# The start of a decoder trunk reordered: x loaded first, products on ones ahead, v's products sorted by part

## The chip, the cores and the metric

The kernel runs on one core of one Trainium2 chip. The metric is the device time of one execution in microseconds (us). Before the change it is 1229.62 us, the median of three runs (1229.15 to 1229.67).

## What is computed

The reference is a trunk of two layers on 512 tokens of width 1024, all in float32. Layer 0 mixes tokens by an attention with forget gates, layer 1 by a gated short convolution; each mixer is followed by a squared-ReLU MLP and a gated per-layer input. Only the very beginning of layer 0 bears on the change:

```python
def rmsnorm(x, g):
    y = x * rsqrt(mean(x * x, axis=-1) + RMS_EPS)
    return y * g

hn = rmsnorm(x, g[0])                 # x: (512, 1024)
proj = hn @ w_attn_in                 # (512, 3*1024 + 16): q, k, v and 16 forget-gate logits
f_logit = proj[..., 3 * D:] + b_f     # 16 heads
```

The order in which q, k, v and the logits are computed is free. The kernel begins with a part of v and the logits.

## The kernel before

**Precision.** TensorE multiplies in a reduced float format (fp32r). To keep float32 accuracy the kernel splits each operand into a high part (rounded by a copy on ScalarE, `wh`, `hTh`) and a low part (what the rounding left, by a subtraction on VectorE or GpSimd, `wl`, `hTl`). `split` (L270) does both. A product is then three: high by high, low rows by high weights, high rows by low weights (`mm3`, L264 to L266).

**Blocks.** The 512 tokens are four blocks of 128 rows (t = 0 to 3), the width is eight blocks of 128 (k = 0 to 7). Each block of x comes as two halves of 128x512 (tiles `xa` for t = 0, `xc` for the others).

**The beginning, per token block.** `stats` squares both halves on ScalarE (L295, with a sum) and calls `rstd` on GpSimd (L287 adds, L290 raises to -1/2). `scaled` (L303) multiplies a half by that and by the gain `g0` on VectorE, giving `n_h`. `turned` (L312) transposes four 128x128 pieces of `n_h` on TensorE into the PSUM tile `n_p`. `keep` splits that into `hTh` (ScalarE) and `hTl` (VectorE), the turned rows. The gain `g0` is a row of 1024 numbers; two products with a one-row stationary of ones (L983) spread it over 128 partitions in PSUM.

**v.** The columns of v and of the logits are computed in three chunks (`V_CHUNKS`): first the last 256 columns of v with the 16 logit columns (272 wide), then 512, then 256. `values(c, t)` computes chunk c for token block t: eight k, three products each. Within it, after five k (`if k == 5 and between`), the next block's rows are turned. `keep_v` moves the result out of PSUM: the logits plus `b_f` on VectorE (L454), then the parts of v as high copies (ScalarE) and low parts (VectorE), one after the other.

**Loads.** `fetch` issues weight loads on SyncE's queue into a ring of 14 `raw` tiles; `prepare(n)` splits the weights up to number n (the first eight are those of the first chunk, 272 wide). `load_x` loads x. Loads complete on a ring of eight semaphores (DMAHW0 to DMAHW7), so the ninth load waits for the first to have landed, and so on.

**Order.** The program is ordered by a scheduler, except where a `manual_schedule` block fixes the order of the named engines as written: the loads (SyncE, ScalarE) and the first chunk of v (TensorE, VectorE, ScalarE). Each engine works through its own queue strictly in order.

## Time and profile before

| | |
|---|---|
| median of three runs | 1229.62 us |
| profiled execution | 1230.79 us |
| its span | 1229.1 us |
| granted clock, mean over the span | 0.997 |
| TensorE busy | 1210.3 us |
| VectorE, ScalarE, GpSimd busy | 912.2, 676.4, 657.1 us |
| instructions | 18662 |

The profile is of one execution. Its span runs from the first to the last instruction on the engines; the execution's own time is a little longer, and lies above the median of the runs beside it. In the rows, PE is TensorE, PEld its weight loads, DVE VectorE, ACT ScalarE, POOL GpSimd, SP SyncE; SPq and ACTq are the queues that issue loads. A row of the timeline gives start, length (us), engine, line, operation, what is written and read, and in brackets how long the engine was idle before and who released it. A group row gives busy time and the mean of one in ns. The lines are those of the kernel before.

### The profile page before, as it was taken

How to read it: one execution, taken by the hardware profiler on the slowest of the kernel's cores; microseconds unless marked ns; L12 is line 12 of the kernel's file. 1: busy time of each engine (PE TensorE's matmuls, PEld its weight loads, DVE VectorE, ACT ScalarE, POOL GpSimd, SP SyncE). 2: the span in 40 equal slices, each digit the busy share in tenths (PEclk: the TensorE clock that was granted, in tenths of full speed). 3: DMA queues.
4: the chain of work that ended last, by engine and by line, in shares of the span. 5: the costliest groups of instructions: out<-in, count | busy, mean ns of one | idle time of the engine just before them, and what ended most of it. 6: DMA issues, size and time to landing. Idle time of an engine off the chain costs nothing.

```text
span 1229.1 us, 18662 instructions
## 1 busy us (share of the span) xinstructions
PE 1210.3 (98%) x6188; PEld 1030.5 (84%) x6188; DVE 912.2 (74%) x1410; ACT 676.4 (55%) x1429; POOL 657.1 (53%) x619
## 2 busy tenths in 40 slices
PE   7999999999999999999999999999999999999997
PEld 6888888898888888888889999989888888888886
DVE  5648878676778767869877798867776787669873
ACT  5447777556744654455565544445756345645551
POOL 2016656244977787775213255316677878678210
PEclk9999999999999999999999999999999999999999
DMA  7456564542343324428133033552422443236401
GB/s 251 149 157 172 143 172 113 167 149 78 103 137 105 98 73 137 132 68 296 57 100 108 30 104 95 156 174 74 137 78 60 137 138 99 64 113 180 162 18 52
DMA packets 85793, 148.73 MB, mean 121 GB/s; under 512 B 10112, under 2 KB 17328, under 8 KB 85696
## 3 DMA queue, kind: packets, MB, share of 16 engines
q1 hardware_dynamic: 85488, 147.27, 39.2%
q8 instruction: 49, 0.80, 0.3%
q14 instruction: 48, 0.39, 0.1%
q10 hardware_dynamic: 144, 0.26, 0.1%
q0 software_dynamic: 64, 0.00, 0.0%
HBM read 136.93 MB, written 6.37 MB: 117 GB/s over the span
## 4 chain that ended last, share of the span: by engine, by line
PE 96%; ACT 1%; DVE 1%; DMA 1%; issue 1%; POOL 1%; SPq 0%; DVEq 0%; POOLq 0%; ACTq 0%
PE up L266 9%; PE up L265 9%; PE up L264 9%; PE dn L264 8%; PE dn L265 8%; PE dn L266 8%; PE qk L265 2%; PE qk L264 2%; PE qk L266 2%; PE pg L265 2%; PE pg L264 2%; PE pg L266 2%; PE n_p L312 1%; PE pT L539 1%; PE v L264 1%; PE v L265 1%
## 5 line engine op out<-in xcount | busy, mean ns | idle before, releaser
L273 DVE TENSOR_TENSOR wl<-raw,wh 128x512 fp32r<-128x512 f32 (+1 forms) x398 | 377.3, 991 | 22.3 <-ACT wh L272 21.3
L272 ACT CAST wh<-raw 128x512 fp32r<-128x512 f32 (+1 forms) x398 | 217.5, 620 | 4.6 <-DVE xd L348 4.4
L265 PE MATMUL up<-hTh,wl 128*128 128x512 f32 (+1 forms) x576 | 210.2, 365 | 0.0
L266 PE MATMUL up<-hTl,wh 128*128 128x512 f32 (+1 forms) x576 | 209.7, 366 | 0.0
L264 PE MATMUL up<-hTh,wh 128*128 128x512 f32 (+1 forms) x576 | 208.7, 366 | 0.0
L820 ACT ACTIVATE r<-up 128x512 f32<-128x512 f32 (+1 forms) x72 | 39.4, 547 | 203.2 <-PE up L266 201.0
L273 POOL TENSOR_TENSOR wl<-dn_T,wh 128x512 fp32r<-128x512 f32 x96 | 132.6, 1413 | 30.1 <-ACT wh L272 30.1
L167 POOL TENSOR_TENSOR dn_T<-raw,raw 128x512 f32<-128x512 f32 x56 | 86.9, 1563 | 68.8 <-DMA raw<-in_wdn 58.3
L265 PEld LDWEIGHTS up<-hTh,wl 128*128 128x128 f32 x576 | 108.6, 189 | 17.5
L264 PEld LDWEIGHTS up<-hTh,wh 128*128 128x128 f32 x576 | 108.6, 189 | 17.6
L266 PEld LDWEIGHTS up<-hTl,wh 128*128 128x128 f32 x576 | 108.3, 189 | 17.5
L866 DVE TENSOR_TENSOR acc<-dn,acc 128x512 f32<-128x512 f32 x168 | 107.3, 679 | 14.9 <-PE dn L266 14.8
L167 POOL TENSOR_TENSOR dn_T<-raw,dn_T 128x512 f32<-128x512 f32 x56 | 92.4, 1650 | 2.2
L272 ACT CAST wh<-dn_T 128x512 fp32r<-128x512 f32 x112 | 61.4, 616 | 11.1 <-POOL dn_T L167 11.1
L273 DVE TENSOR_TENSOR A12l<-q,A12h 128x512 fp32r<-128x512 f32 x28 | 22.4, 801 | 55.0 <-ACT A12h L272 54.9
L880 POOL TENSOR_TENSOR acc<-acc,acc 128x512 f32<-128x512 f32 x28 | 46.9, 1706 | 9.9 <-DVE acc L866 9.9
L265 PE MATMUL qk<-hTh,wl 128*128 128x512 f32 x128 | 51.0, 399 | 0.0
L266 PE MATMUL qk<-hTl,wh 128*128 128x512 f32 x128 | 51.0, 398 | 0.0
L264 PE MATMUL qk<-hTh,wh 128*128 128x512 f32 x128 | 50.9, 398 | 0.0
L265 PE MATMUL pg<-wh,hTl 128*128 128x512 f32 x128 | 50.5, 394 | 0.0
L264 PE MATMUL pg<-wh,hTh 128*128 128x512 f32 x128 | 50.4, 394 | 0.0
L273 DVE TENSOR_TENSOR A11l<-q,A11h 128x256 fp32r<-128x256 f32 x28 | 23.1, 825 | 36.5 <-ACT A11h L272 36.5
(371 smaller groups left out, 3244.4 us busy)
## 6 DMA issues: line engine op xcount, KB each, us to landing
raw<-in_wup SPq DMA_DIRECT2D x128, 256.0 KB, 2.9
raw<-in_wdn SPq DMA_DIRECT2D x128, 256.0 KB, 2.8
raw<-in_wcq SPq DMA_DIRECT2D x36, 256.0 KB, 2.8
raw<-in_wqk SPq DMA_DIRECT2D x32, 256.0 KB, 3.4
raw<-in_wpg SPq DMA_DIRECT2D x32, 256.0 KB, 4.3
g<-in_g SPq DMA_DIRECT2D x22, 256.0 KB, 5.3
prl<-neg_c SPq DMA_DIRECT2D x16, 256.0 KB, 6.7
raw<-in_wo SPq DMA_DIRECT2D x16, 256.0 KB, 5.9
```

Of the source, the lines that this page charges most:

```text
L167: ins = nc.gpsimd.tensor_tensor(out=B[name], in0=B[a], in1=B[b], op=op)
L264: nc.tensor.matmul(ps, a.hi, b.hi, start=start, stop=False)
L265: nc.tensor.matmul(ps, a.lo, b.hi, start=False, stop=False)
L266: nc.tensor.matmul(ps, a.hi, b.lo, start=False, stop=stop)
L272: nc.scalar.copy(hi, src)
L273: return eng.tensor_tensor(out=lo, in0=src, in1=hi.bitcast(F32), op=ALU.subtract)
L312: nc.tensor.transpose(ps[:, j * P : (j + 1) * P], h[:, j * P : (j + 1) * P], ident)
L539: nc.tensor.transpose(ps[:, b * P : (b + 1) * P], probs[h][b][:, j * P : (j + 1) * P], ident)
L820: nc.scalar.activation(r[:, :n], ps[:, :n], AF.Relu)
L866: ins = nc.vector.tensor_tensor(out=a, in0=banks[s], in1=a, op=ALU.add)
L880: nc.gpsimd.tensor_tensor(out=a, in0=a, in1=acc[i, s][:, :S], op=ALU.add)
```

## The change

Only the beginning is touched, to the end of the first chunk of v, and `keep_v`.

- The load of `b_f` moves from the head of SyncE's queue to behind all of x. The two rows of the gain go from GpSimd's queue to ScalarE's, behind x's half there.
- A tile `warm` is set to one on VectorE, and `work(n)` issues n products of it with itself into a PSUM bank that nobody reads: eleven ahead of the gain's products, two between the two turned halves of block 0.
- Of the two halves that a mean of squares needs, ScalarE squares the first and VectorE the second (`products`, a product with a sum that starts at EPS); VectorE adds the two and GpSimd raises to -1/2 (`mean_squares`, `inverse`).
- The low parts of weights 2 and 3, 4 to 6, and 8 to 13 are computed on GpSimd rather than VectorE (`prepare(..., nc.gpsimd)`).
- In the first chunk the products are sorted by part: for k = 0 to 3 high by high, high rows by low weights, low rows by high weights; for k = 4 to 7 high by high, low rows, then (after the next block's rows are turned) low weights.
- `keep_v` issues all high copies first and then all low parts; the evacuation of block t is placed behind the products of block t + 1, and behind the scaled rows of later blocks.

SyncE's queue at the program's start, with what a load waits for, before and now (`xa` is x's block 0, `xc` with the lower numbers is block 1, `raw` are weights of v):

```order
L604 DMA b_f<-in_bf 128x16
L357 DMA xa_0_93<-in_x 128x512
L157 DMA raw_97<-in_wv 128x272
L157 DMA raw_99<-in_wv 128x272
L157 DMA raw_101<-in_wv 128x272
L157 DMA raw_103<-in_wv 128x272
L357 DMA xc_0_105<-in_x 128x512
L357 DMA xc_1_106<-in_x 128x512 [waits DMAHW0_49]
L157 DMA raw_109<-in_wv 128x272 [waits DMAHW1_49]
```
```order
L365 DMA xa_0_93<-in_x 128x512
L157 DMA raw_99<-in_wv 128x272
L157 DMA raw_101<-in_wv 128x272
L157 DMA raw_103<-in_wv 128x272
L157 DMA raw_105<-in_wv 128x272
L365 DMA xc_0_107<-in_x 128x512 [waits DMAHW0_49]
L365 DMA xc_1_108<-in_x 128x512 [waits DMAHW1_49]
L157 DMA raw_111<-in_wv 128x272 [waits DMAHW2_49]
L157 DMA raw_113<-in_wv 128x272 [waits DMAHW3_49]
```

`b_f` is gone from the front, and the loads of x's block 1 now wait for semaphores that block 0's loads hold (ScalarE's three loads take semaphores of the same ring).

ScalarE's queue at the start, before and now (`junk,n_q` are the squares with their sum, `wh` casts of weights, `hTh` casts of turned rows of block 0):

```order
L357 DMA xa_1_94<-in_x 128x512
L295 ACT_TABLE_LOAD
L295 ACTIVATE junk,n_q_0_155<-xa_0_93 128x512
L295 ACTIVATE junk,n_q_0_157<-xa_1_94 128x512
L272 CAST wh_163<-raw_97 128x272
L272 CAST wh_167<-raw_99 128x272
L272 CAST wh_171<-raw_101 128x272
L272 CAST wh_179<-raw_103 128x272
L272 CAST hTh<-n_p_0_183 128x4x128
L272 CAST wh_190<-raw_109 128x272
```
```order
L365 DMA xa_1_94<-in_x 128x512
L1023 DMA row_89<-in_g 1x512
L1023 DMA row_90<-in_g 1x512
L295 ACT_TABLE_LOAD
L295 ACTIVATE junk,n_q_0_172<-xa_0_93 128x512
L272 CAST wh_181<-raw_99 128x272
L272 CAST wh_185<-raw_101 128x272
L272 CAST wh_189<-raw_103 128x272
L272 CAST wh_193<-raw_105 128x272
L295 ACTIVATE junk,n_q_1_201<-xc_0_107 128x512
L272 CAST hTh<-n_p_0_208 128x4x128
L272 CAST hTh<-n_p_1_217 128x4x128
```

One square of block 0 left; the square of block 1 (`n_q_1`) stands ahead of block 0's `hTh` casts, and no weight is cast between those two any more.

VectorE around the third and fourth token block, before and now (`n_h` scaled rows of block 3, `hTl` low turned rows, `logit` block 0's logits, `v_3` low parts of v):

```order
L303 SCALAR_TENSOR_TENSOR n_h_0_284<-xc_0_121,n_r_y,g_0_126 128x512
L303 SCALAR_TENSOR_TENSOR n_h_1_286<-xc_1_122,n_r_y,g_1_127 128x512
L273 TENSOR_TENSOR hTl<-n_p_0_304,hTh 128x4x128
L273 TENSOR_TENSOR hTl<-n_p_1_311,hTh 128x4x128
L273 TENSOR_TENSOR wl_328<-raw_329,wh_327 128x512
L273 TENSOR_TENSOR wl_334<-raw_335,wh_333 128x512
L273 TENSOR_TENSOR wl_340<-raw_341,wh_339 128x512
L454 TENSOR_TENSOR logit<-v_0_237,b_f 128x16
L273 TENSOR_TENSOR v_3_135<-v_0_237,v_3_135 128x2x64 x2
```
```order
L311 SCALAR_TENSOR_TENSOR n_h_0_358<-xc_0_123,n_r_305,g_0_130 128x512
L311 SCALAR_TENSOR_TENSOR n_h_1_360<-xc_1_124,n_r_305,g_1_131 128x512
L470 TENSOR_TENSOR logit<-v_0_255,b_f 128x16
L485 TENSOR_TENSOR v_3_153<-v_0_255,v_3_153 128x2x64 x2
L273 TENSOR_TENSOR hTl<-n_p_0_400,hTh 128x4x128
L273 TENSOR_TENSOR hTl<-n_p_1_407,hTh 128x4x128
L470 TENSOR_TENSOR logit<-v_1_319,b_f 128x16
```

The low splits of 512-wide weights are gone from here, and the logits of block 0 stand directly behind block 3's scaled rows; the high copies of v on ScalarE wait for them.

```diff
--- before.py
+++ after.py
@@ -171,7 +171,7 @@
                     mybir.DependencyInfo(mybir.DependencyClass.Sync, mybir.DependencyReason.DATA),
                 )
 
-    def prepare(upto):
+    def prepare(upto, lows=None):
         while begun[0] < min(upto, len(order)):
             n = begun[0]
             begun[0] += 1
@@ -185,7 +185,7 @@
                 eng = nc.gpsimd if (key[0] == "dn" and key[2] > 0) or key[-1] in ON_POOL else nc.vector
             else:
                 fetch(at + 1)
-                raw, eng, w = fetched[at], nc.vector, loads[at].shape[-1]
+                raw, eng, w = fetched[at], lows or nc.vector, loads[at].shape[-1]
                 fetched[at] = None
             split(hi[:, :w], lo[:, :w], raw[:, :w], eng)
             ready[key] = Pair(hi[:, :w], lo[:, :w])
@@ -295,6 +295,14 @@
         nc.scalar.activation(junk, src, AF.Square, scale=D**-0.5, accum_out=ss)
         return ss
 
+    def products(src, name):
+        ss = stat(name)
+        nc.vector.tensor_tensor_reduce(
+            out=page(f"{name}_sq")[:, :S], in0=src, in1=src, scale=1.0 / D, scalar=EPS,
+            op0=ALU.mult, op1=ALU.add, accum_out=ss,
+        )
+        return ss
+
     def stats(t, xs, name):
         return rstd([squares(xs[n][:, :S], f"{name}_q{n}_{t}") for n in range(2)], f"{name}_r{t}")
 
@@ -385,9 +393,7 @@
                          f"{kind}r")
                 then(t)
 
-    def attention(hT, first_x, g0, by_hand):
-        b_f = consts.tile([P, H], F32, tag="bf", name="b_f")
-
+    def attention(hT, first_x, g0, b_f, work, by_hand):
         vs = [[page(f"v{t}_{i}", F32R) for i in range(4)] for t in range(NB)]
         n_f = NB * H
         logit = stat("logit", n_f)
@@ -435,7 +441,7 @@
                 )
                 nc.sync.dma_start(neg_c[b, :, :n], t[:H, :n])
 
-        def values(c, t, soon=SOON, between=None):
+        def values(c, t, mid=None):
 
             c0, width = V_CHUNKS[c]
             n_v = min(width, D - c0)
@@ -444,10 +450,20 @@
                 if width == 256:
                     w = wide("v", c, k // 2).at(lambda u: u[:, k % 2 * 256 : k % 2 * 256 + 256])
                 else:
-                    w = wide("v", c, k, soon=soon)
-                if k == 5 and between:
-                    between()
-                mm3(ps[:, :width], tokens(hT, k, t), w, k == 0, k == KT - 1)
+                    w = wide("v", c, k, soon=0 if mid else SOON)
+                if not mid:
+                    mm3(ps[:, :width], tokens(hT, k, t), w, k == 0, k == KT - 1)
+            HH, LH, HL = ("hi", "hi"), ("lo", "hi"), ("hi", "lo")
+            for n in range(2 if mid else 0):
+                for part, of in (HH, HL, LH) if n == 0 else (HH, LH, HL):
+                    if n and of == "lo":
+                        mid()
+                    for k in range(4 * n, 4 * n + 4):
+                        nc.tensor.matmul(
+                            ps[:, :width], getattr(tokens(hT, k, t), part),
+                            getattr(ready["v", c, k], of),
+                            start=k == 0 and part == of, stop=k == KT - 1 and of == "lo",
+                        )
 
             def keep_v():
                 if n_v < width:
@@ -455,13 +471,20 @@
                         out=logit[:, t * H : (t + 1) * H], in0=ps[:, n_v:width], in1=b_f,
                         op=ALU.add,
                     )
+                splits = []
                 for c1 in range(0, n_v, 256):
                     src = ps[:, c1 : c1 + 256].rearrange("p (i e d) -> p i e d", e=2, d=HD)
                     block = vs[t][(c0 + c1) // 256].rearrange("p (i r) -> p i r", i=2)
                     for e in range(2):
                         hi = block[:, :, 192 * e : 192 * e + HD]
                         lo = block[:, :, 64 + 64 * e : 128 + 64 * e]
-                        split(hi, lo, src[:, :, e, :])
+                        splits.append((hi, lo, src[:, :, e, :]))
+                for hi, _, src in splits:
+                    nc.scalar.copy(hi, src)
+                for hi, lo, src in splits:
+                    nc.vector.tensor_tensor(
+                        out=lo, in0=src, in1=hi.bitcast(F32), op=ALU.subtract
+                    )
 
             return keep_v
 
@@ -601,37 +624,60 @@
             prepare(where["o", 1, KT - 1] + 1)
             yield from out_part((0, 1), (6,))
 
-        nc.sync.dma_start(b_f, bf[0:1, :].partition_broadcast(P))
         name = "n0"
         E, done_v = mybir.EngineType, []
 
-        def rows(t):
-            r = stats(t, first_x[t], name)
+        def mean_squares(t):
+            half = lambda n: first_x[t][n][:, :S]
+            q = squares(half(0), f"{name}_q0_{t}"), products(half(1), f"{name}_q1_{t}")
+            v = stat(f"{name}_v{t}")
+            nc.vector.tensor_tensor(out=v, in0=q[0], in1=q[1], op=ALU.add)
+            return v
+
+        def inverse(t, v):
+            r = stat(f"{name}_r{t}")
+            nc.gpsimd.tensor_tensor(out=r, in0=v, in1=neg_half, op=ALU.pow)
+            return r
+
+        def scale_rows(t, r):
             return [scaled(t, n, first_x[t], r, g0, name) for n in range(2)]
 
         def turn_rows(t, hs):
             for n in range(2):
                 keep(t, n, turned(t, n, hs[n], name), hT)
 
-        with tc.manual_schedule(engines={E.PE, E.DVE, E.Activation}):
-            r = stats(0, first_x[0], name)
-            prepare(3)
-            hs = {0: [scaled(0, n, first_x[0], r, g0, name) for n in range(2)]}
-            prepare(4)
-            for n in range(2):
-                keep(0, n, turned(0, n, hs[0][n], name), hT)
-                prepare(5 + n)
+        with tc.manual_schedule(engines={E.PE, E.DVE, E.Activation, E.Pool}):
+            r = inverse(0, mean_squares(0))
+            prepare(2)
+            prepare(4, nc.gpsimd)
+            hs = scale_rows(0, r)
+            v = mean_squares(1)
+            ps0 = turned(0, 0, hs[0], name)
+            keep(0, 0, ps0, hT)
+            work(2)
+            ps0 = turned(0, 1, hs[1], name)
+            keep(0, 1, ps0, hT)
+            r = inverse(1, v)
+            prepare(KT - 1, nc.gpsimd)
+            hs1 = scale_rows(1, r)
             prepare(KT)
-            hs[1] = rows(1)
-            hs[2] = rows(2)
-            for t in range(NB):
-                between = (lambda: turn_rows(t + 1, hs[t + 1])) if t + 1 < NB else None
-                done_v.append(values(0, t, 0, between))
-                if t + 3 < NB:
-                    hs[t + 3] = rows(t + 3)
-                if t:
-                    prepare(KT + 3 * t)
-                    done_v.pop(0)()
+            v = mean_squares(2)
+            r = inverse(2, v)
+            done_v.append(values(0, 0, lambda: turn_rows(1, hs1)))
+            v = mean_squares(3)
+            hs2 = scale_rows(2, r)
+            r = inverse(3, v)
+            prepare(KT + 2, nc.gpsimd)
+            done_v.append(values(0, 1, lambda: turn_rows(2, hs2)))
+            hs3 = scale_rows(3, r)
+            done_v.pop(0)()
+            prepare(KT + 4, nc.gpsimd)
+            done_v.append(values(0, 2, lambda: turn_rows(3, hs3)))
+            done_v.pop(0)()
+            prepare(KT + 6, nc.gpsimd)
+            done_v.append(values(0, 3, lambda: None))
+            done_v.pop(0)()
+            prepare(KT + 8)
         done_v.pop(0)()
         tri = page("tri", F32R)
         ones = page("ones")
@@ -967,24 +1013,35 @@
                 then(t)
 
 
-    one = page("one")
+    one, warm = page("one"), page("warm", F32R)
     nc.vector.memset(one[:1, :P], 1.0)
+    nc.vector.memset(warm[:, :S].bitcast(F32), 1.0)
     rows = [page(f"row{n}") for n in range(2)]
-    for n in range(2):
-        nc.gpsimd.dma_start(rows[n][:1, :], g[0:1, n * S : (n + 1) * S])
     with tc.manual_schedule(engines={mybir.EngineType.SP, mybir.EngineType.Activation}):
         first_x = [load_x("xa", 0)]
+        for n in range(2):
+            nc.scalar.dma_start(rows[n][:1, :], g[0:1, n * S : (n + 1) * S])
         fetch(4)
         first_x.append(load_x("xc", 1))
         fetch(KT)
         first_x += [load_x("xc", t) for t in (2, 3)]
+        b_f = consts.tile([P, H], F32, tag="bf", name="b_f")
+        nc.sync.dma_start(b_f, bf[0:1, :].partition_broadcast(P))
     g0 = [bank(f"g0_{n}") for n in range(2)]
-    for n in range(2):
-        nc.tensor.matmul(g0[n], one[:1, :P], rows[n][:1, :], start=True, stop=True)
+    warm_p = bank("warm_p")
+
+    def work(n):
+        for _ in range(n):
+            nc.tensor.matmul(warm_p, warm[:, :P], warm[:, :S], start=True, stop=True)
+
+    with tc.manual_schedule(engines={mybir.EngineType.PE}):
+        work(11)
+        for n in range(2):
+            nc.tensor.matmul(g0[n], one[:1, :P], rows[n][:1, :], start=True, stop=True)
     kept = dram.tile([2, NB, 2, P, S], F32, tag="kept", name="kept")
     hT = turned_x
     by_hand = ExitStack()
-    lhs, opened = attention(hT, first_x, g0, by_hand)
+    lhs, opened = attention(hT, first_x, g0, b_f, work, by_hand)
     oT = lhs
     lhs = lambda k, t: tokens(oT, k, t)
     kind = "o"
```

## Prediction

> **What bounds the kernel now.** I read the page first (busy shares), then TensorE's waits, then its rows over the first 30 us, then the other engines' rows there.
>
> ```profile
> PE 1210.3 (98%) x6188; PEld 1030.5 (84%) x6188; DVE 912.2 (74%) x1410; ACT 676.4 (55%) x1429; POOL 657.1 (53%) x619
> ```
>
> TensorE is busy in 98% of the span, so only its idle time and its slow stretches can be won. The waits, longest first (who waited, for whom, us in total, times, longest):
>
> ```profile
> PE g L983 <- DMA row<-in_g: 6.4, 1, 6.4
> PE n_p L312 <- DVE n_h L303: 1.8, 1, 1.8
> PE ps_o L557 <- DVE pl L273: 0.9, 1, 0.9
> ```
>
> The two large ones stand at the start; the next is 0.9 us, in code that the change leaves as it is. TensorE by stretch (length, busy time with instructions, granted clock, DMA share, GB/s):
>
> ```profile
> 11.83:28.33 16.50, 14.52 (x98) 0.90 0.76 261
> 28.33:47.80 19.47, 19.47 (x99) 1.00 0.64 196
> ```
>
> From 28.33, where the first product of v's last token block starts, TensorE is full until well past the change. So the forecast is one number: when does TensorE reach that product after the change? Its rows up to there (start, us, operation):
>
> ```profile
> 6.37 3.75 PE L983 MATMUL g<-row,one 1*128 1x512 f32 x4 [6.37 <-DMA row<-in_g]
> 10.04 2.03 PE L312 MATMUL n_p<-ident,n_h 128*128 128x128 f32 x8
> 11.83 0.59 PE L264 MATMUL v<-wh,hTh 128*128 128x272 f32 x1
> ...
> 13.18 0.43 PE L264 MATMUL v<-wh,hTh 128*128 128x272 f32 x1
> 13.40 0.42 PE L265 MATMUL v<-wh,hTl 128*128 128x272 f32 x1
> ...
> 13.78 0.29 PE L264 MATMUL v<-wh,hTh 128*128 128x272 f32 x1
> ...
> 14.78 0.29 PE L266 MATMUL v<-wl,hTh 128*128 128x272 f32 x1
> ...
> 16.91 1.84 PE L312 MATMUL n_p<-ident,n_h 128*128 128x128 f32 x8 [1.84 <-DVE n_h L303]
> ...
> 28.33 0.63 PE L264 MATMUL v<-wh,hTh 128*128 128x272 f32 x2
> ```
>
> Two products that follow each other start 0.22 us apart at 13.2; from 13.78 to 14.78 there are eight such steps, 0.125 us each: the same instruction at half clock and at full clock. Eight transposes likewise take 2.03 and 1.84 us here, and 0.87 us in the chain of waits at 22.60:
>
> ```profile
> 22.60 0.87 PE n_p L312 x8
> ```
>
> The granted clock says when it fell:
>
> ```profile
> 17.00:18.00 1.00, 1.00 (x6) 0.55 1.05 399
> 20.00:21.00 1.00, 1.00 (x8) 0.75 1.06 369
> ```
>
> It drops near 17.1, behind an idle time of 1.84 us, and returns near 20.5; by the pace of the products it had first risen near 13.7. The three points lie 3.4 us apart. I read this as a clock decided anew every 3.4 us from TensorE's work just before. Half a stretch idle (13.7 to 17.1) cost the clock; the stretch before 10.3, filled by the one-row products on g, did not raise it. At full clock, 72 products (9.0 us) and 24 transposes (2.6 us) make 11.6 us; the stretch 11.83 to 28.33 took 16.5. That is 4.9 us of loss to win there, plus whatever moves the 11.83.
>
> **The way to the first product of v.** What ends last is x's tile, then squares, the power, scaling, turning, and the cast.
>
> ```profile
> 0.80 0.39 SPq L604
> 1.24 4.41 DMA xa<-in_x
> ```
> ```profile
> 5.67 0.63 ACT L295 ACTIVATE junk<-xa 128x512 f32<-128x512 f32 x1 [3.15 <-DMA xa<-in_x]
> 6.21 0.19 ACT L295 ACTIVATION_READ_ACCUMULATOR junk<-xa 128x1 f32 x1
> 6.42 0.63 ACT L295 ACTIVATE junk<-xa 128x512 f32<-128x512 f32 x1
> ```
> ```profile
> 7.25 0.30 POOL L287 TENSOR_SCALAR n_r_v<-n_q,n_q 128x1 f32<-128x1 f32 x1 [4.21 <-ACT junk L295]
> 7.63 0.73 POOL L290 TENSOR_TENSOR n_r_y<-n_r_v,neg_half 128x1 f32<-128x1 f32 x1
> ...
> 21.74 0.53 POOL L638 MEMSET ones<- 128x512 f32 x1
> ```
> ```profile
> L526 DVE CUSTOM_DVE_ANT_0 prl<-sc,prl 128x512 f32<-128x512 f32 x16 | 11.0, 687 | 4.4 <-PE pT L539 2.6 <-PE sc L524 1.1 <-DMA raw<-in_wo 0.7
> L531 DVE RECIPROCAL rs<-sm 128x1 f32<-128x1 f32 x64 | 10.1, 157 | 8.0 <-ACT prr L530 6.0 <-ACT prl L530 1.2 <-ACT pr L530 0.3
> ```
>
> The load of b_f leaves SyncE's queue ahead of x, so x is issued at 0.80 instead of 1.24 and lands at 5.65 - 0.44 = 5.2. Both squares ran on ScalarE, to 7.14. Now the second runs on VectorE beside the first: ScalarE's ends at 5.2 + 0.73 = 5.95, VectorE's, priced as the product-and-reduce of the same shape, at 5.2 + 0.69 + 0.1 for reading the sum (what ScalarE's reading adds) = 6.0. No row has both operands in SBUF with a sum; the dear end is a 1.41 us row below. The addition is at most the 0.157 us of a 128x1 operation: 6.2. The power (0.73) ends at 7.0; it was 8.36. The 0.30 us on GpSimd is gone.
>
> Scaling also waits for g. Before, the rows landed at 6.37 and the four passes held TensorE until 10.1, and the second scaled half waited 0.86 us for them. Now eleven products on ones stand ahead. They wait for a 128x512 memset, which GpSimd does in 0.53; from about 1.0 on VectorE that is 1.5. At 0.22 us each (128x512 at full clock: the 19.47 us stretch less 3 us for block 3's 24 products, over the other 75) to 0.39 (times 0.22/0.125), they end between 4.0 and 5.8; I take 5.0, the clock rising at 3.5 since the points repeat every 3.4. The rows of g now go behind x's half on ScalarE's queue; I put them at 5.6 and 6.0, not before x (5.2) and hardly after the old 6.4. At full clock, g takes 1.9 us instead of 3.75, in part at half clock 2.3: the first half at 6.6, the second at 8.0. The first scaled half (0.74) then ends at 7.9, the second at 8.9; turning starts at 8.0.
>
> Here the change adds a wait. ScalarE's square for the second x block is now ahead of the first casts of turned rows, which are what the first product needs:
>
> ```profile
> 3.60 1.41 SPq L357 DMA_DIRECT2D xc<-in_x  x2
> ```
> ```profile
> raw<-in_wup SPq DMA_DIRECT2D x128, 256.0 KB, 2.9
> ```
> ```profile
> xc<-in_x SPq DMA_DIRECT2D x6, 256.0 KB, 4.1
> ```
> ```profile
> 11.20 0.58 ACT L272 CAST hTh<-n_p 128x512 fp32r<-128x512 f32 x1 [2.78 <-PE n_p L312]
> ```
>
> That block's load was issued at 3.60. Now ScalarE's two rows of g take places in the ring of eight completion semaphores, so the load waits until x's first tile has landed: 5.2. With the queue nearly empty I use 2.9 us to landing (busy median: 4.1): 8.2. The square holds ScalarE to 9.0, the cast (0.58) ends at 9.7. TensorE is no earlier: in the stretch 6.9 to 10.3 it has gaps and g's one-row passes, so I expect half clock there: eight transposes 1.8 us and two products on ones 0.9 from 8.0, with the wait for the second scaled half inside, give **10.55** for the first product, 1.3 us earlier than 11.83.
>
> **From the first product to the last block.** The order by part needs only high parts for four products, then low weights, then low rows. VectorE's low splits of weights move to GpSimd:
>
> ```profile
> L273 POOL TENSOR_TENSOR wl<-dn_T,wh 128x512 fp32r<-128x512 f32 x96 | 132.6, 1413 | 30.1 <-ACT wh L272 30.1
> L834 POOL TENSOR_TENSOR s<-s,q 128x256 f32<-128x256 f32 x28 | 29.4, 1049 | 2.2
> L834 POOL TENSOR_TENSOR s<-q,s 128x256 f32<-128x256 f32 x28 | 21.4, 765 | 2.2
> ```
>
> For 272 columns I take 0.75, from the 128x256 rows (0.77 to 1.05); the dear end is the 1.41 of 512. Two are done by 8.7 and three by 14.0, where they are needed at 11.3 and 14.3: hidden, with a margin of 0.3 us on the last; at 1.41 they would cost 1.2. The six 512-wide ones take 8.5 us from 17.3 on. TensorE wants the last near 32, so they too are hidden; at 1.75 it would still be so.
>
> ```profile
> 16.11 2.91 DVE L303 SCALAR_TENSOR_TENSOR n_h<-xc,n_r_y,g 128x512 f32<-128x512 f32 x4 [1.60 <-POOL n_r_y L290]
> 18.93 1.28 DVE L273 TENSOR_TENSOR hTl<-n_p,hTh 128x512 fp32r<-128x512 f32 x2
> ```
> ```profile
> L760 DVE TENSOR_TENSOR z<-c,us 128x512 f32<-128x512 f32 x6 | 8.2, 1412 | 0.0
> ```
> ```profile
> 26.90 0.27 ACT L272 CAST v<-v 128x128 fp32r<-128x128 f32 x1 [1.20 <-DVE logit L454]
> 24.03 1.67 ACT L272 CAST wh<-raw 128x512 fp32r<-128x512 f32 x3
> ```
>
> Now VectorE sets the pace: per token block two low splits (1.28 a pair, 0.6 apart), two scaled halves (2.91 for four, 0.72 apart) and a product-and-reduce with its sum and addition (0.95). Walking the queues: low splits of block 0 end near 12.0 (the second waits for its cast at 11.3), scaled block 1 at 13.4, low splits of block 1 at 15.9, scaled block 2 at 16.7 and 17.4. TensorE, at full clock from 10.3, waits 0.3 us for the casts of the weights' second four, then 0.2 and 0.25 for block 2's scaled rows. The last wait is the new order of v's evacuation: the high copies wait for the logits, as the 1.20 us row shows they did before, and the logits now stand behind block 3's scaled rows, at 21.6. Behind them on ScalarE are two copies (to 22.05), two 512-wide casts (0.55 each, to 23.2) and block 3's first turned cast, 23.75; TensorE has been ready since 22.95, so it waits **0.85**. Sum: 11.6 + 0.3 + 0.45 + 0.85 = 13.2 us, so the first product of block 3 starts at 10.55 + 13.2 = **23.8** against 28.33: 4.5 us. A product-and-reduce beside GpSimd may be dearer (its two-operand neighbours reach the 1.41 above); at 1.41 for all four the walk loses 1.5. I take 0.2 off: **4.3 us**.
>
> **Behind that** the same products follow in nearly the same order, and block 3 is done earlier among them, so the logits' chain has no less time than before. The copies and low parts of v, now in two groups, lie beside products on which nothing waits. b_f is issued near 9.7 and needed at 21.4. The thirteen products on ones cost nothing where they fill waits. Span 1229.1 - 4.3 = 1224.8. The profiled execution took 1230.8, 1.7 over its span; the median 1229.62 lies 1.2 under it: 1229.6 - 4.3 = **1225.3**.
>
> **Rivals.** (1) *The clock stays up once raised.* If the gaps and g's passes between 5.0 and 10.3 do not cost it, turning takes 0.9 and the first product is bound by the cast at 9.7: 2.1 us won there, 5.7 in all, 1223.9. Against it is the drop at 17.1 after 1.84 us idle. The Trainium skill ("TensorE: Matmul & The Clock Gate", "Why this matters for your kernels") speaks for it: it asks only that gaps stay under about 3 us. The trace's 1.84 us with a lost clock disagrees. Chance 0.2.
> (2) *The clock comes late.* If transposes do not count as work, half clock lasts until 13.7: twenty-four products and eight transposes at 0.1 us more are 3.2 us, of which VectorE's pace hides two thirds: gain 3.2, 1226.4. The dear VectorE price and g's rows at 6.4 (gain 2.5 to 3.0) end near there. Chance 0.19.
> (3) *It is slower: the head-of-line wait on ScalarE.* Once x's second block lands later than about 9, the delay goes through the square and the cast to the first product and through VectorE's product to all that follows, every later load is issued later too, and an idle TensorE gets its full clock a stretch later. By the walk, landing at 9.2 loses 0.1 to 0.7, at 12.2 nothing of the gain is left, and at 14 the time is 1231. That is 7 us from issue to landing to break even; the busy median is 4.1. Chance 0.06.
> (4) *No gain:* what TensorE wins up front it waits for later, on GpSimd's 512-wide splits or casts. They have 3 us of cover by the walk: 1229. Chance 0.09.
>
> **How the numbers follow.** My forecast (1224.7 to 1225.9) has 0.46. The range runs from below rival 1 through rival 2, 1223.2 to 1227.2, and leaves out 3 and 4. A measurement tells about 0.2% (2.5 us) from no change: my case, 1 and 2 are faster, 0.85; rival 4 is the same, 0.09; rival 3 slower, 0.06.
>
> **What would show it.** Right: products on ones from about 1.5; x's square at 5.2; first product of v near 10.5 at 0.125 us pace; waits of TensorE before block 3's casts; that block near 23.8; all later rows the same 4 to 5 us earlier. Wrong: half clock in the rows after 10.3 (rival 2), ScalarE idle for x's second block beyond 9 (3), new waits of TensorE on low parts of weights between 24 and 48 (4).

## The result, and the profile after

| | before | after |
|---|---|---|
| median of ten runs | 1229.64 us (1229.15 to 1231.64) | 1225.87 us (1225.33 to 1228.51) |
| profiled execution | 1230.79 us | 1226.43 us |
| its span | 1229.1 us | 1224.7 us |

The ratio of the two is 0.997, with a 95% interval from 0.9961 to 0.998. The change saves 3.8 us, 0.3%. The gain is small, but the interval leaves out 1. The prediction was 1225.3 us, with a range from 1223.2 to 1227.2 and a span of 1224.8.

The busy shares of the changed kernel, from the head of its page:

```profile
PE 1212.2 (99%) x6201; PEld 1032.4 (84%) x6201; DVE 915.1 (75%) x1412; ACT 672.0 (55%) x1421; POOL 665.5 (54%) x624
```

TensorE is busy 1.9 us longer, with 5.8 us of products on ones added (rows below), and still ends 4.4 us earlier. What it waits for in the changed kernel (for whom, us in total, times, longest):

```profile
PE warm_p L1035 <- DVE warm L1018: 1.6, 1, 1.6
PE ps_o L580 <- DVE pl L273: 0.9, 1, 0.9
...
PE v L462 <- ACT hTh L272: 0.4, 1, 0.4
```

The 6.4 us for g's rows and the 1.8 us for block 1's scaled rows are gone. New are 1.6 us for the tile of ones and 0.4 us for a cast of turned rows. TensorE's own rows up to the first product of block 3 (start, length, operation):

```profile
1.63 5.06 PE L1035 MATMUL warm_p<-warm 128*128 128x512 f32 x11 [1.63 <-DVE warm L1018]
6.62 1.99 PE L1040 MATMUL g<-row,one 1*128 1x512 f32 x4
8.66 0.66 PE L320 MATMUL n_p<-ident,n_h 128*128 128x128 f32 x4
9.07 0.71 PE L1035 MATMUL warm_p<-warm 128*128 128x512 f32 x2
...
9.99 1.21 PE L462 MATMUL v<-wh,hTh 128*128 128x272 f32 x4
...
18.29 1.38 PE L320 MATMUL n_p<-ident,n_h 128*128 128x128 f32 x8
...
22.52 1.04 PE L320 MATMUL n_p<-ident,n_h 128*128 128x128 f32 x8
23.32 0.75 PE L462 MATMUL v<-wl,hTh 128*128 128x272 f32 x4
24.46 0.78 PE L462 MATMUL v<-wh,hTh 128*128 128x272 f32 x4 [0.40 <-ACT hTh L272]
```

The first product of v starts at 9.99 (before: 11.83), block 3's first product at 24.46 (before: 28.33). Of these 3.9 us, 1.8 are won ahead of v and 2.0 within its first three blocks. The stretches (length, busy time with instructions, granted clock, DMA share, GB/s) and, below them, single microseconds:

```profile
9.99:24.46 14.47, 13.87 (x100) 0.88 0.99 347
24.46:43.94 19.48, 19.48 (x96) 1.00 0.63 192
```
```profile
9.00:10.00 1.00, 1.00 (x10) 1.00 1.04 299
10.00:11.00 1.00, 1.00 (x6) 0.54 1.10 303
...
13.00:14.00 1.00, 1.00 (x8) 0.75 0.83 246
14.00:15.00 1.00, 1.00 (x12) 1.00 1.03 395
```

The part behind block 3's first product is as long as before (19.47 us to the sums of the logits), so what was won stays won. But the clock fell once more: from about 10.1 to 13.5 TensorE ran at half clock, over v's first products.

### The profile page after: what moved, and what is told of

The parts are those of the page before. It is cut to its first block, busy times and chain, and to the rows that moved or that the text cites. A ratio compares the mean times of both kernels' runs of the same rounds, so it can differ in the third digit from the quotient of the medians.

```text
span 1224.7 us, 18700 instructions
## 1 busy us (share of the span) xinstructions
PE 1212.2 (99%) x6201; PEld 1032.4 (84%) x6201; DVE 915.1 (75%) x1412; ACT 672.0 (55%) x1421; POOL 665.5 (54%) x624
## 3 DMA queue, kind: packets, MB, share of 16 engines
HBM read 136.93 MB, written 6.37 MB: 117 GB/s over the span
## 4 chain that ended last, share of the span: by engine, by line
PE 94%; DVE 2%; ACT 1%; issue 1%; POOL 1%; POOLq 0%; DVEq 0%; ACTq 0%
PE up L264 9%; PE up L266 9%; PE up L265 9%; PE dn L264 8%; PE dn L266 8%; PE dn L265 8%; PE qk L265 2%; PE qk L264 2%; PE qk L266 2%; PE pg L264 2%; PE pg L265 2%; PE pg L266 2%; PE pT L562 1%; PE n_p L320 1%; PE co L264 1%; PE co L266 1%
## 5 line engine op out<-in xcount | busy, mean ns | idle before, releaser
L266 PE MATMUL pg<-wl,hTh 128*128 128x512 f32 x128 | 50.2, 392 | 0.0
```

Source lines behind the costliest of these rows:

```text
L266: nc.tensor.matmul(ps, a.hi, b.lo, start=False, stop=stop)
```

## The experiments

The prediction's account goes into the runs: the gain comes from an earlier start and from producers that are ready sooner (VectorE relieved of low splits, squares and scaled rows issued early); the clock, read on a grid of 3.4 us, takes part of it away. The runs undo or isolate one part each, and each expectation below names its own theory A and rival B.

All results in one table. The runs were made on several chips, so each median stands beside that of the kernel before on the same chip. The last three columns are from the profiled execution: starts of v's first product and of block 3's first product, and the stretch at half clock once TensorE had work for v.

| kernel | median, us (range, n) | before beside it | ratio (95%) | v | block 3 | half clock |
|---|---|---|---|---|---|---|
| the change | 1225.87 (1225.33-1228.51, 10) | 1229.64 | 0.9970 (0.9961-0.9980) | 9.99 | 24.46 | 10.1-13.5 |
| no_ones | 1226.53 (1225.60-1228.68, 10) | 1229.72 | 0.9976 (0.9967-0.9986) | 10.53 | 24.45 | to 12.7 |
| full_g | 1225.42 (1225.19-1226.49, 5) | 1229.72 | 0.9966 (0.9953-0.9979) | 9.89 | 23.52 | none |
| old_order | 1225.62 (1225.49-1229.02, 9) | 1229.72 | 0.9971 (0.9961-0.9980) | 9.99 | 23.81 | 9.1-12.5 |
| lows_on_vector | 1227.02 (1226.59-1229.77, 10) | 1229.72 | 0.9982 (0.9973-0.9992) | 10.06 | 25.00 | 8.0-11.4 |
| before_with_ones | 1229.89 (1228.17-1231.34, 10) | 1230.37 | 0.9995 (0.9986-1.0004) | 12.00 | 28.79 | 8.2-15.0, 18.4-21.8 |
| x_late | 1226.68 (1225.66-1228.50, 7) | 1230.37 | 0.9972 (0.9961-0.9983) | 10.33 | 24.26 | 9.1-12.5 |
| logits_later | 1225.16 (1224.82-1227.64, 5) | 1230.37 | 0.9964 (0.9951-0.9977) | 10.10 | 23.17 | none |
| full_g_logits | 1224.66 (1224.28-1225.01, 4) | 1230.37 | 0.9956 (0.9939-0.9973) | 10.11 | 23.18 | none |
| squares_on_scalar | 1225.54 (1225.24-1226.16, 6) | 1229.75 | 0.9969 (0.9957-0.9981) | 9.99 | 23.62 | 8.4-11.8 |
| full_g_logits_8 | 1223.63 (1223.50-1223.89, 4) | 1229.75 | 0.9953 (0.9937-0.9970) | 8.91 | 22.06 | none |
| before_rows_early | 1228.73 (1228.43-1229.70, 10) | 1229.75 | 0.9993 (0.9984-1.0003) | 11.92 | 25.82 | to 15.3 |
| before_again | 1229.92 (one run) | 1230.50 (one run) | - | 11.46 | 27.06 | to 15.3 |

An interval reaches about 1.2 us to each side with nine or ten runs and 2.1 us with four. An edit worth less than that is settled by its trace or not at all. A trace settles it only where the clock is alike: half clock lay over v's products for 3.4 us in the change, for 1.3 to 2.5 us in no_ones, old_order, lows_on_vector, x_late and squares_on_scalar, and not at all in full_g, logits_later and the two kernels that join them. full_g below shows 0.9 us at block 3 for the 3.4 us.

### no_ones: the change without products on ones

```diff
     def work(n):
-        for _ in range(n):
+        for _ in range(0):
             nc.tensor.matmul(warm_p, warm[:, :P], warm[:, :S], start=True, stop=True)
```

> The change without its thirteen products on ones. Theory A (the gain is the producers' path: squares on two engines, sorted products, low splits on GpSimd; the ones only serve g's passes and the turning of block 0): g starts near 5.5 at half clock and holds TensorE to about 9.2, first product near 10.9 instead of 9.99, half clock to 13.5 as with the ones; block 3's first product at 24.8 to 25.4 (24.46 with the ones), time 0.3 to 0.9 us over the change. Rival B (the ones are the gain, by the clock): block 3 past 26.5, at least 2 us over the change.

TensorE's rows in it:

```profile
5.05 3.75 PE L1040 MATMUL g<-row,one 1*128 1x512 f32 x4 [5.05 <-DMA row<-in_g]
8.73 2.03 PE L320 MATMUL n_p<-ident,n_h 128*128 128x128 f32 x8
10.53 0.60 PE L462 MATMUL v<-wh,hTh 128*128 128x272 f32 x1
...
24.45 0.77 PE L462 MATMUL v<-wh,hTh 128*128 128x272 f32 x4 [0.40 <-ACT hTh L272]
```

Without the ones g's passes start when its rows land, at 5.05, but take 3.75 us at half clock and end at about the same time as in the change. The first product comes 0.5 us later, block 3's first product at the same time, with half clock over v for 2.2 us instead of 3.4; both are earlier than expected, where half clock was to last to 13.5. By the medians, each against its own before, the ones are worth 0.6 us (3.8 less 3.2), inside the interval. The eleven products also delay g: in the change they run to 6.6, and by this trace g's rows had landed 1.6 us earlier. Against the kernel before, g's passes and the turning of block 0 are as long as they were (3.75 and 2.03 us); g's rows land at 5.05 instead of 6.37, and v starts 1.3 us earlier with them.

### full_g: g spread by products of full height

```diff
-    nc.vector.memset(one[:1, :P], 1.0)
+    nc.vector.memset(one[:, :P], 1.0)
+    for n in range(2):
+        nc.gpsimd.memset(rows[n][:, :S], 0.0)
-            nc.tensor.matmul(g0[n], one[:1, :P], rows[n][:1, :], start=True, stop=True)
+            nc.tensor.matmul(g0[n], one[:, :P], rows[n][:, :S], start=True, stop=True)
```

> The change with g spread by full-height products (a stationary of ones on all 128 rows; the other 127 rows of the moving operand are zero), so that only the height of the four passes differs. Theory A (one-row passes do not count as work for the clock): the fall of the clock near 10.1 goes, first products of v 0.125 us apart, block 3's first product at 23.6 to 23.9, time 0.6 to 0.9 us under the change. Rival B (passes count by time, the fall comes from the gaps): the clock falls near 10.1 all the same, block 3 at 24.4 to 24.6.

The other 127 rows are zero. TensorE's rows for the high products of block 0's second four k, and from block 2's turning on:

```profile
11.50 0.96 PE L462 MATMUL v<-wh,hTh 128*128 128x272 f32 x4
...
17.35 1.38 PE L320 MATMUL n_p<-ident,n_h 128*128 128x128 f32 x8 [0.39 <-DVE n_h L311]
...
23.52 0.65 PE L462 MATMUL v<-wh,hTh 128*128 128x272 f32 x3 [0.40 <-ACT hTh L272]
```

The clock did not fall, and block 3's first product came 0.94 us earlier. Half clock for 3.4 us costs 1.7 us of TensorE's work; half of that shows, because a faster TensorE waits longer: 0.3 us for the casts of weights (the next products start 0.79 us behind them, where four take 0.5) and 0.3 more for block 2's scaled rows (0.39 us idle, 0.12 in the change). By the medians full_g saves 4.3 us against 3.8: in theory A's direction, within the interval.

### old_order: the products per k, as before

```diff
-            for n in range(2 if mid else 0):
-                for part, of in (HH, HL, LH) if n == 0 else (HH, LH, HL):
...
+            for k in range(KT if mid else 0):
+                if k == 5:
+                    mid()
+                for part, of in (HH, LH, HL):
```

> The change with the first chunk's products in the order of before (three per k, next block turned after five k). Theory A (sorting saves waits for low rows): each block's second product waits for low rows, about 0.9 us in block 0 and 0.3 to 0.6 in the others; block 3 at 25.0 to 26.0, time 0.5 to 1.5 us over the change. Rival B (VectorE sets the pace whatever TensorE's order is): block 3 within 0.3 us of 24.46.

Its first two products, block 1's turning and block 3's first product:

```profile
9.99 0.57 PE L461 MATMUL v<-wh,hTh 128*128 128x272 f32 x1
10.54 0.60 PE L461 MATMUL v<-wh,hTl 128*128 128x272 f32 x1
...
13.30 1.04 PE L320 MATMUL n_p<-ident,n_h 128*128 128x128 f32 x8
...
23.81 0.33 PE L461 MATMUL v<-wh,hTh 128*128 128x272 f32 x1
```

Block 3 is 0.65 us earlier than in the change, outside both expectations, and the gain is 4.1 us against 3.8. Part of the 0.65 can be the clock (half clock over v for 2.5 us instead of 3.4). Sorting the products by part brings nothing that these runs show, against the prediction's use of it ("The order by part needs only high parts for four products"). The second product does wait for low rows (0.55 us behind the first, where the pace at half clock is 0.23), but block 3 is not later for it. The edit also moves the turning: 15 products of a block stand ahead of it instead of 20, and block 1 is turned at 13.30 instead of 14.13, so its rows reach the other engines earlier. Sorting with the turning left in its place was not run.

### lows_on_vector: VectorE keeps the low splits of weights

```diff
-                raw, eng, w = fetched[at], lows or nc.vector, loads[at].shape[-1]
+                raw, eng, w = fetched[at], nc.vector, loads[at].shape[-1]
```

> The change with all low parts of weights on VectorE, at the same places of the program. Theory A (VectorE sets the pace from 10 to 24): five 272-wide splits (0.36 each) and four 512-wide ones (0.6) come back into its queue ahead of block 3's low rows; block 3 at 26.5 to 28.5, time 2 to 4 us over the change. Rival B (VectorE has slack): under 0.5 us over the change.

Its first copies of v on ScalarE, and block 3's first product:

```profile
22.99 0.43 ACT L483 CAST v<-v 128x128 fp32r<-128x128 f32 x2 [2.81 <-DVE logit L470]
```
```profile
25.00 0.77 PE L462 MATMUL v<-wh,hTh 128*128 128x272 f32 x4 [0.83 <-ACT hTh L272]
```

The splits delay the logits on VectorE, the copies start at 22.99 instead of 22.45, and TensorE waits 0.83 instead of 0.40 us. The gain falls from 3.8 to 2.7 us, a difference no larger than an interval's half; the trace carries it, since block 3 is 0.54 us later although half clock lay over v for 1.3 us only. The mechanism is theory A's; its price of 2 to 4 us was too high.

### before_with_ones: the kernel before, with the products on ones

```diff
-    for n in range(2):
-        nc.tensor.matmul(g0[n], one[:1, :P], rows[n][:1, :], start=True, stop=True)
+    with tc.manual_schedule(engines={mybir.EngineType.PE}):
+        work(11)
+        for n in range(2):
+            nc.tensor.matmul(g0[n], one[:1, :P], rows[n][:1, :], start=True, stop=True)
...
                 keep(0, n, turned(0, n, hs[0][n], name), hT)
+                if n == 0:
+                    work(2)
```

> The kernel before plus the thirteen products on ones, nothing else. Theory A (without earlier producers a better clock only waits longer): g's passes end near 8.5 instead of 10.1, first product of v 1 us earlier, but the idle time before block 1's turning ends at 16.1 to 16.9 as before, so block 3's first product is at 27.3 to 28.4 and the time within 1 us of before. Rival B (the clock is the gain): block 3 under 26.3, at least 2 us under before.

TensorE's turning of block 1, and three single microseconds:

```profile
17.19 1.31 PE L312 MATMUL n_p<-ident,n_h 128*128 128x128 f32 x8 [1.72 <-DVE n_h L303]
```
```profile
14.00:15.00 1.00, 1.00 (x6) 0.50 1.05 395
...
19.00:20.00 1.00, 1.00 (x6) 0.50 1.05 378
21.00:22.00 1.00, 1.00 (x6) 0.59 1.05 387
```

Alone they bring 0.5 us by the medians, with 1 inside the interval. x is not earlier, the wait for block 1's scaled rows is about as long as before (1.72 and 1.84 us), and the clock fell twice. What they bring goes with the clock: the four runs with a mean granted clock of 0.997 or 0.998 took 1228.2 to 1228.5 us, the six with 0.993 to 0.996 took 1229.8 to 1231.3.

### x_late: `b_f` ahead of x, the rows of g on GpSimd's queue

```diff
+    for n in range(2):
+        nc.gpsimd.dma_start(rows[n][:1, :], g[0:1, n * S : (n + 1) * S])
     with tc.manual_schedule(engines={mybir.EngineType.SP, mybir.EngineType.Activation}):
+        b_f = consts.tile([P, H], F32, tag="bf", name="b_f")
+        nc.sync.dma_start(b_f, bf[0:1, :].partition_broadcast(P))
         first_x = [load_x("xa", 0)]
-        for n in range(2):
-            nc.scalar.dma_start(rows[n][:1, :], g[0:1, n * S : (n + 1) * S])
```

> The change with the load of b_f back at the head of SyncE's queue and the two rows of g back on GpSimd's. Theory A (in the change TensorE's ones and g's passes end last, not x: the power is ready at 6.46, the first half of g near 7.6): x lands 0.4 us later without effect, x's block 1 is issued earlier again; block 3's first product within 0.4 us of 24.46, time within 0.5 us of the change. Rival B (x's lead is on the path): 0.4 to 0.8 us over the change.

ScalarE's square of x's first block starts at 5.68 in it, against 4.45 in the change. That square, the power and the scaled rows:

```profile
5.68 0.63 ACT L295 ACTIVATE junk<-xa 128x512 f32<-128x512 f32 x1 [3.16 <-DMA xa<-in_x]
```
```profile
6.75 0.87 POOL L639 TENSOR_TENSOR n_r<-n_v,neg_half 128x1 f32<-128x1 f32 x1 [3.71 <-DVE n_v L634]
```
```profile
7.65 1.42 DVE L311 SCALAR_TENSOR_TENSOR n_h<-xa,n_r,g 128x512 f32<-128x512 f32 x2
```

The half of x on SyncE's queue comes 1.2 us later, the power is ready at 7.62 instead of 6.46, and yet block 3's first product starts at 24.26, no later than in the change, and the gain is 3.7 us against 3.8. Here the scaled rows do follow the power, not g (its first half is ready near 7.3), and v starts at 10.33, 0.34 us later than in the change and in old_order, whose clock fell at the same 9.1; half clock over v for 2.2 us instead of 3.4 can hide that at block 3. So with eleven products on ones ahead, the lead of x is worth about 0.3 us at most, which the medians do not show.

### logits_later: block 0's evacuation behind block 3's turned rows

```diff
             hs3 = scale_rows(3, r)
+            done_v.append(values(0, 2, lambda: turn_rows(3, hs3)))
             done_v.pop(0)()
             prepare(KT + 4, nc.gpsimd)
-            done_v.append(values(0, 2, lambda: turn_rows(3, hs3)))
```

> The change with block 0's evacuation and two weight splits placed behind block 3's turned rows instead of ahead of them, so that ScalarE casts those rows before it waits for the logits. Theory A (the wait before block 3 is that head-of-line wait): the 0.40 us wait before block 3's first product goes, block 3 at 24.0 to 24.1, time 0.3 to 0.5 us under the change. Rival B (VectorE's scaled rows bound it, or GpSimd's 512-wide splits start too late and TensorE waits for them): block 3 at 24.0 but the time as in the change or longer, with new waits between 26 and 34.

ScalarE's casts of block 3's turned rows in it:

```profile
22.42 1.07 ACT L272 CAST hTh<-n_p 128x512 fp32r<-128x512 f32 x2 [2.86 <-PE n_p L320]
```

They start at 22.42, released by TensorE, where the change has them at 23.81 behind copies of v and two weight casts. The 0.40 us wait is gone, and block 3 starts at 23.17. This profile has no fall of the clock either, though g's passes are one row high, so the 1.29 us between the two traces are the wait and the clock together; the expected 24.0 was for the wait alone. Against full_g, which kept its clock too, the stretch from v to block 3 is 13.07 us instead of 13.63: 0.56 us are the wait. The gain is 5.2 us against 3.8.

### full_g_logits and full_g_logits_8: both together, then eight products on ones

The first joins the edits of full_g and logits_later; the second also has `work(8)` in place of `work(11)`.

> Full-height products for g and the later logits together. Theory A: both gains add, since one lies at 10 to 13.5 and the other at 24: block 3's first product at 23.0 to 23.5, time 1.0 to 1.4 us under the change. Rival B (one bound hides the other): no more than the better one of the two alone.

> Full-height g, later logits, and eight products on ones instead of eleven. Theory A (in the change the last ones and g's passes, not x, hold block 0's scaling back: the power is ready at 6.46, the first half of g at 7.6): g starts near 5.3, the first scaled half starts 0.5 to 0.9 us earlier, block 3's first product at 22.3 to 22.9, time 1.3 to 2.0 us under the change. Rival B (fewer ones leave the clock at half rate until later and g's passes eat the gain): block 3 at 23.1 or later, no better than with eleven.

TensorE's rows with eight:

```profile
1.64 3.78 PE L1037 MATMUL warm_p<-warm 128*128 128x512 f32 x8 [1.64 <-DVE warm L1018]
5.22 2.04 PE L1042 MATMUL g<-row,one 128*128 128x512 f32 x4
...
8.91 0.77 PE L462 MATMUL v<-wh,hTh 128*128 128x272 f32 x4
...
22.06 0.67 PE L462 MATMUL v<-wh,hTh 128*128 128x272 f32 x4
```

With both edits the gain is 5.7 us. Whether the two gains add is not settled: block 3 starts at 23.18, as in logits_later, whose profile kept its clock too, and the medians' 0.5 us between them lie inside the interval. Three products on ones fewer start g 1.3 us earlier, v 1.2 us earlier and block 3 1.1 us earlier: 1223.63 us, 6.1 us under the kernel before beside it. Its slowest run (1223.89) is under the fastest of the change (1225.33, on another chip whose before is 0.1 us lower). It is the best version found, and shows that TensorE, held by the eleven products, was what ended last ahead of g. With eight, the power is ready at 6.28 and the first half of g near 6.2, so fewer still would start the scaled rows no sooner.

### before_rows_early: the kernel before, with the producers' order alone

```diff
             prepare(4)
+            r1 = stats(1, first_x[1], name)
             for n in range(2):
...
-            hs[1] = rows(1)
-            hs[2] = rows(2)
+            hs[1] = [scaled(1, n, first_x[1], r1, g0, name) for n in range(2)]
+            r2 = stats(2, first_x[2], name)
             for t in range(NB):
...
+                if t == 0:
+                    hs[2] = [scaled(2, n, first_x[2], r2, g0, name) for n in range(2)]
```

> The kernel before, with only the places of two things changed: block 1's squares stand ahead of block 0's turned casts, and block 2's scaled rows behind block 1's turned ones. Theory A (what the change won is mainly that block 1's rows are ready when TensorE wants to turn them; before, its squares stood behind eight weight casts): the idle time of 1.84 us before block 1's turning shrinks to under 0.8, the clock does not fall for lack of work there, block 3's first product at 25.2 to 26.2 instead of 28.33, time 2 to 3 us under before. Rival B (GpSimd's splits, the sorting and the second square on VectorE carry it): block 3 past 27.2, under 1.2 us gained.

TensorE's rows for block 1's turning and block 3's first product:

```profile
15.70 1.04 PE L312 MATMUL n_p<-ident,n_h 128*128 128x128 f32 x8
...
25.82 0.63 PE L264 MATMUL v<-wh,hTh 128*128 128x272 f32 x2
```

The idle time ahead of block 1's turning is gone, the clock does not fall behind it, and block 3 starts 2.5 us earlier than in the first profile of before. The medians differ by 1.0 us only, with 1 inside the interval. Trace and time disagree here; the second profile of before, below, says why.

### squares_on_scalar: both squares on ScalarE, as before

```diff
-            q = squares(half(0), f"{name}_q0_{t}"), products(half(1), f"{name}_q1_{t}")
+            q = squares(half(0), f"{name}_q0_{t}"), squares(half(1), f"{name}_q1_{t}")
```

> The change with both squares of each block on ScalarE again (the sum of the two and EPS stays on VectorE). Theory A (TensorE's ones and g's passes end last at the start, and VectorE sets the pace after it): block 0's power is 0.75 us later and still ready ahead of g; VectorE has 0.77 us less per block; block 3's first product at 24.0 to 24.8 and the time within 0.4 us of the change. Rival B (the second square on VectorE is what moves the start): 0.7 us or more over the change, first product of v past 10.6.

v starts at 9.99 as in the change, block 3 at 23.62 (half clock over v for 1.8 us instead of 3.4), and the gain is 4.2 us against 3.8: dividing the squares between two engines brings nothing that these runs show.

### before_again: the kernel before, profiled once more

> The kernel before, unchanged, for a second profiled execution. In the profiles so far the clock's 3.4 us grid stood at a different phase in nearly every execution. Theory A (the phase is free, and the profiled execution of before was one in which the clock fell at a bad moment, which is why it lies 1.2 us over its median): the falls and rises lie elsewhere, block 3's first product moves by 0.3 us or more from 28.33, and the span by the same amount. Rival B (the phase is set by the program's start, and the difference between that execution and the median is something else): fall at 17.0 to 17.1 and rise at 20.5 again, block 3 at 28.2 to 28.5.

TensorE's rows in the second profile of before:

```profile
5.99 3.75 PE L983 MATMUL g<-row,one 1*128 1x512 f32 x4 [5.99 <-DMA row<-in_g]
...
16.55 1.31 PE L312 MATMUL n_p<-ident,n_h 128*128 128x128 f32 x8 [0.94 <-DVE n_h L303]
...
27.06 0.63 PE L264 MATMUL v<-wh,hTh 128*128 128x272 f32 x2
```

The same program starts block 3 at 27.06, not 28.33. g's rows landed 0.4 us earlier; half clock lasted to about 15.3 instead of 13.7, so TensorE reached block 1's turning later, waited 0.94 instead of 1.84 us, and kept its clock behind that. Block 3 moved by 1.27 us, the span by 0.9 (1228.2), not by the same amount. The first profile, at 1230.79 us, was 1.2 us over its median, and this difference accounts for most of it. Against this profile before_rows_early is 1.2 us ahead at block 3, which agrees with its 1.0 us.

## Why the prediction was right, and where its steps were wrong

**The size.** 4.3 us were predicted; the two profiled spans differ by 4.4, the medians by 3.8. The chain was as described: TensorE was to reach block 3 earlier and then run full, which it did. That the span came within 0.1 us is in part luck: v started 0.6 us earlier than forecast and the stretch from there to block 3 took 1.3 us longer, so that 3.9 us were won at block 3, and another 0.5 us came behind it, where the prediction put nothing. Two of its sums do not come out either: 8.0, 1.8 and 0.9 make 10.7 for the start of v, not 10.55, and rival 1's 2.1 us with the 3.3 us of the main sum (16.5 less 13.2) make 5.4, not 5.7. Rivals 3 and 4 did not come: x's second block landed by 7.8, and no new wait of TensorE appears behind 24.46. ScalarE's rows answer rival 3:

```profile
4.45 0.63 ACT L295 ACTIVATE junk<-xa 128x512 f32<-128x512 f32 x1 [1.12 <-DMA xa<-in_x]
...
7.79 0.63 ACT L295 ACTIVATE junk<-xc 128x512 f32<-128x512 f32 x1 [1.35 <-DMA xc<-in_x]
...
9.35 0.59 ACT L272 CAST hTh<-n_p 128x512 fp32r<-128x512 f32 x1 [0.83 <-PE n_p L320]
...
22.45 0.43 ACT L483 CAST v<-v 128x128 fp32r<-128x128 f32 x2 [2.15 <-DVE logit L470]
```

The square of block 1 (7.79) waited for its load and was over by 8.5; the first cast of turned rows, at 9.35, waited 0.83 us for TensorE, not for that square. The head-of-line wait exists and costs nothing here.

**x and the power.** x was put at 5.2 and came at about 4.4 (the square on ScalarE at 4.45, VectorE's at 4.68 below). The step that failed is "lands at 5.65 - 0.44": the new order of the loads saved 1.2 us there, not only the issue time of `b_f`. x_late, which puts `b_f` and g's rows back together, takes the 1.2 us away again; which of the two does it was not tested. The power was ready at 6.46, not 7.0. It mattered little, as x_late shows. VectorE's and then GpSimd's rows in the changed kernel:

```profile
4.68 0.69 DVE L300 CUSTOM_DVE_ANT_0 n_q_sq<-xa 128x512 f32<-128x512 f32 x1 [3.11 <-DMA xa<-in_x]
...
7.85 1.54 DVE L311 SCALAR_TENSOR_TENSOR n_h<-xa,n_r,g 128x512 f32<-128x512 f32 x2 [1.46 <-POOL wl L273]
```
```profile
5.81 0.65 POOL L639 TENSOR_TENSOR n_r<-n_v,neg_half 128x1 f32<-128x1 f32 x1 [4.45 <-DVE n_v L634]
6.43 1.46 POOL L273 TENSOR_TENSOR wl<-raw,wh 128x272 fp32r<-128x272 f32 x2
...
23.48 2.54 POOL L273 TENSOR_TENSOR wl<-raw,wh 128x512 fp32r<-128x512 f32 x2 [2.80 <-ACT wh L272]
```

The product-and-reduce took 0.69 us, the end that was taken, so the 0.2 us set aside for a dear one were not needed. GpSimd's 272-wide split took 0.73 us (0.75 taken), the 512-wide one 1.27 (1.41 taken), and TensorE waits for none of them. VectorE's wait of 1.46 us at 7.85 is put down to GpSimd's split (`wl`); the power had been ready since 6.46, and TensorE's first pass on g ended near 7.6, so it was g.

**The start of v.** "they end between 4.0 and 5.8; I take 5.0, the clock rising at 3.5" failed: all eleven products on ones ran at half-clock pace (0.43 us each) to 6.6, and the clock rose near 6.7. The first scaled half began at 7.85, when it was to have ended. Against that, turning ran at full clock, where half was expected (8.66 to 9.99 with the two products on ones), and v started at 9.99 instead of 10.55. Two errors of opposite sign.

**The pace to block 3.** The 13.2 us from 10.55 failed by their size: it took 14.5 from 9.99. Worked out again from the changed kernel's rows: 11.6 us of work at full clock, as predicted; 1.7 for 3.4 us at half clock; 0.6 for block 2's scaled rows (its turning starts 0.28 late at 18.29 and is 0.34 longer than block 3's); 0.55 ahead of block 3 (23.32 to 24.46 is 1.14, the same step in logits_later 0.59). Sum 14.45. The waits were put at 1.6 and were 1.2; what was missing is the clock ("at full clock from 10.3"). In full_g, which kept its clock, the stretch took 13.6 us, 0.4 over the prediction, and the 0.3 us for the casts of weights, hidden in the change by half clock, are there. The half clock came one step of the grid later than predicted: rival 2's half clock until 13.7 was right, though not its reason, since TensorE had been at full clock before.

**The last wait.** Two copies, two 512-wide casts and block 3's first turned cast behind the logits are what the trace shows: logits 22.25, copies 22.45, casts 22.77, turned rows 23.81, TensorE 24.46. logits_later, which takes that queue apart, has no wait. Predicted 0.85, measured 0.55.

**Where the gain comes from.** By undoing one part at a time, by the medians: low splits on GpSimd 1.1 us, ones 0.6, x's lead and the queue of g's rows 0.1, sorting and the second square on VectorE nothing (both kernels without them were 0.3 to 0.4 us ahead). By doing one part alone: the producers' order 1.0, the ones 0.5. Each of these is smaller than an interval's half, and they sum to less than 3.8. The parts depend on each other and on where the clock's grid falls: the ones and the earlier rows of g stand in for each other, since without ones the rows bring 1.3 of the 1.8 us ahead of v (no_ones), and with ones late rows and a late x cost 0.34 us there (x_late). How the rest of the 3.8 us divides was not isolated. The forecast "VectorE sets the pace" is right in kind (lows_on_vector) but the price was too high.

**One profile as the base.** The 1.84 us wait and the fall behind it were taken as the kernel's own; the second profile has half of that wait and no such fall. The difference at block 3 is 3.9 us against the one and 2.6 against the other, while those two spans differ from the change's by 4.4 and 3.5: 0.5 to 0.9 us arise behind block 3. They move between executions of one program too (259.4 to 287.6 in before_again against 261.0 to 288.7 in the first profile, from the first `up` product to the first `dn` product).

## What to carry to other kernels

Filling TensorE ahead of its first real work can pay only up to the moment at which its operands land: count the filling by what arrives when, not by a round number (with eight products block 3 started 1.1 us earlier than with eleven). When an engine's queue holds the evacuation of an old tile ahead of what the next product needs, move the evacuation back before looking at how operands are ordered. And where a start-up stretch depends on a clock that is decided on a grid, take two profiles of the kernel before subtracting anything from one.

## What the runs showed of the hardware that was not expected

- The grid of 3.4 us has no fixed phase against the program. In five kernels that differ by an edit, with v starting at 9.99 to 10.33, the fall came at 10.1, 9.1, 8.0, 9.1 and 8.4, and the rise 3.4 us behind each. In the two profiles of the kernel before, the pace rose near 13.7 and near 15.3.
- The clock fell at 10.1 in the changed kernel though TensorE had no idle time of 0.1 us between 1.63 and that moment. What stood in the 3.4 us before were g's one-row passes (2.0 us), transposes and two products on ones. Of the kernels with ones ahead, those with full-height passes on g (three of three) kept their clock; with one-row passes it fell in six, counting one of before with ones, and held in logits_later. So the height of the passes is suspected and not shown. The Trainium skill ("TensorE: Matmul & The Clock Gate", "Why this matters for your kernels") ties a return to the low clock to idle gaps of over about 3 us; this trace disagrees, with a fall at under 0.1 us of idle time.
- The granted clock reads 1.00 ahead of the first change on record even where the pace is half: in no_ones eight transposes take 2.03 us at 8.73, twice the 1.04 us of the changed kernel at 22.52, and the stretch behind it reads (granted clock in the fourth column):

```profile
9.00:10.00 1.00, 1.00 (x6) 1.00 1.03 280
```

Up to that first change the pace of equal instructions tells the clock, not this column.
